# A hybrid decoder layer: the set-up, the order of the sample's queries, two planner numbers, one place of the memory change and the last pass are rewritten

## The chip, the core and the metric

The kernel runs on one core of one Trainium2 chip. The metric is the device time of one execution in microseconds (us). The kernel before took 823.68 us, the median of three runs (823.04 to 825.53). The profile is of another execution of the same program.

The engines are named as the profile names them: PE is TensorE with its matmuls (PEld its weight loads), DVE is VectorE, ACT ScalarE, POOL GpSimd, SP SyncE, which here only issues transfers. A name with q behind it (SPq) is that engine's sequencer.

## The reference, cut to what matters

One step of one layer for 512 prompt tokens and, at the same time, for 8 sample sequences of 4 new tokens each, which look back on 4096 cached tokens. All of it is fp32.

```python
hn = rms_norm(x, norm_mix)                      # x: 512 or 32 rows of 1024
z = hn @ w_in                                   # 1024 x 2560: q, k, v, u, gv of 512 each
q, k = rms_norm(z[:, q], q_gain), rms_norm(z[:, k], k_gain)     # groups of 64
att = softmax_1(q k) v - lam * softmax_2(q k) v # causal; the sample reads its cache through page_table
mix = gelu(u) * (tril(w_spatial) @ rms_norm(gelu(gv), gv_gain) + b_spatial)
h = x + concat(rms_norm(att, subln_gain) * (1 - lam_init), mix) @ w_out
y = h + square(relu(rms_norm(h, norm_ffn) @ w_up)) @ w_down     # D_FF 4096
```

Outputs are y for prompt and sample, and the new k, v and gv rows.

## The kernel before, in words

**Number format.** PE multiplies in a reduced fp32 (`fp32r`). For full precision each weight tile of 512 x 256 (512 KB, called raw when it lands) is split by `w_conv` (L265) into a high part (`wh`, a copy on ACT) and a low part (`wl`, a subtraction on DVE), and the activations are kept as `Thi` and `Tlo`; each product is three matmuls, high by high, high by low, low by high. The 32 sample rows, packed as high and low side by side in `spk`, go through PE in "packed" matmuls of 64 rows. Raw tiles are asked for by `w_issue`, at most `RAWB` = 3 ahead in a list written out beforehand; `w_get` hands out the next split pair. The first four weights are the two halves (512 of the 1024 rows each) of the two q pieces.

**Stages.** `setup` (L395) loads, builds the identity `idt` and small index columns, computes the page indices `idxK`, and issues the first two gathers of the key cache. `in_proj` (L836) multiplies ten column pieces of 256, two each for q, k, v, u, gv; for each it goes through the four prompt tiles of 128 tokens (`optB`, 12 matmuls of 256 columns for one tile and one weight half) and the packed sample. Before the first piece each prompt tile has to be multiplied by the gain (`x_gain`, L715), transposed on PE (8 transposes of 128 x 128) and split (`x_tile`, L718). Prompt attention follows inside the later pieces and behind them, then the output projection, then the feed-forward net in eight groups of 512 columns (`ffn`, L1153): the prompt runs alone through the first five (groups 0 to 4), the sample joins for the rest. `second_phase` (L117) gives the memory of the cache part to more weight buffers; before, it is called between groups 3 and 4. `finish` (L1236) transposes a result of 256 columns back and scales the rows.

**The sample's cache** runs beside all that. 64 chunks of keys and 64 of values are gathered by POOL's indirect transfers into two raw key buffers (`kraw`, 1 MB each) and four value buffers. `k_tr` (L563) transposes a key chunk on DVE into `kt` and issues the gather of the chunk two further on; `scores` (L583) multiplies it with the zero-padded queries `qz`, which `qz_fill` (L572) fills once per sample; softmax and the product with the values follow `LAG` chunks later.

**What sets the order.** The list `micro` (L670 to L698) holds these cache steps with weights, and `pump` (L703) calls them as the main work advances: each `yield` in the main work gives a cost, and `TAU` (L700) is the cost of one unit. `ATTW` (L36) is the cost that one step of prompt attention gives. Within this written order a scheduler may still shift instructions; under `pinned(True)` (L384) every engine keeps the written order, without it DVE and PE may move an instruction by at most 28 places, and POOL keeps it always. Each engine then executes its own list strictly in order; a matmul, copy or gather waits for what it needs while everything behind it on that engine waits too. `keep_warm` (L389) issues matmuls on the identity whose result nobody reads.

Of the kernel before, what the change touches and what calls it, by code (L numbers as in the profile page):

```python
# [35 lines left out]
ATTW = 2.4  # L36
# [26 lines left out]
def kernel(  # L63
# [88 lines left out]
    wq = big.tile([128, 4 * T], F32R, tag="r3", name="wq")[:, 0:2048].rearrange("p (s k c) -> p s k c", s=2, k=4)  # L152
# [4 lines left out]
    xg = [R[0][:, 1024 * t:1024 * t + 1024] for t in range(2)]  # L157
# [77 lines left out]
    for g in range(NG):  # L235
        add(group_pieces(g), [wo_pieces()] if g == G1 - 1 else [group_pieces(j) for j in samples(g)] if g >= G1 else (),
            2 if g == NG - 1 else 1)
# [27 lines left out]
    def w_conv():  # L265

        i = st["done"]
        if raws:
            raw = raws.pop(0)
            if i == 3:  # L270
                hi, lo = wq[:, 0], wq[:, 1]
            else:
                pool = pools["w"] if i % 5 > 2 else wp
                hi = pool.tile([128, 4, 256], F32R, tag="wh", name="wh")
                lo = pool.tile([128, 4, 256], F32R, tag="wl", name="wl")
# [119 lines left out]
    def setup():  # L395
        kt0 = kvp.tile([128, 4096], F32, tag="kt", name="kt0")
        xs = kt0[0:32, 0:1024]
        gm = kvp.tile([128, 1024], F32, tag="pp", name="gm")
        fg = kvp.tile([128, 2048], F32, tag="v", name="fg", bufs=VB)
        junk = kvp.tile([128, 512], F32, tag="om", name="junk")  # L400
        ptb = zt_().bitcast(I32).rearrange("p (n q) -> p n q", q=4)
# [11 lines left out]
        for t in range(1, 4):  # L413
            SP.dma_start(out=xt[t], in_=xp[:, t, :])

        G.memset(mhalf, -0.5)
        for t in ssb + [cst]:
            G.memset(t, 1.0)
        kw = dict(base=0, channel_multiplier=0, allow_small_or_imprecise_dtypes=True)
        G.iota(pf[:, 7:8], pattern=[[0, 1]], base=0, channel_multiplier=1, allow_small_or_imprecise_dtypes=True)  # L420
        make_identity(nc, idt)
# [7 lines left out]
        G.memset(gsrc[0:32, :], 0.0)  # L429


        pinned(True)
        for half in range(2):
# [13 lines left out]
        for k in range(8):  # L447
            PE.transpose(ps[:, 32 * k:32 * k + 32], xsg[:, 128 * k:128 * k + 128], idt[:32, :32])
# [969 lines left out]
```

## Time and profile before

| | |
|---|---|
| median of three runs | 823.68 us (823.04 to 825.53) |
| the profiled execution | 822.46 us |
| its span, first to last instruction | 820.7 us |
| PE busy | 797.2 us, 97% |
| DVE busy | 536.3 us, 65% |
| ACT busy | 359.9 us, 44% |
| POOL busy | 181.6 us, 22% |
| HBM | 266 GB/s over the span |

The durations in this document come from the one profiled execution. Its span is what the views divide up; the rest of its time lies around the span. A window's row gives the busy time of each engine in that stretch. A timeline row gives the start and the length of one instruction, or of a run of like ones (x16 is sixteen), and in brackets how long the engine was idle before it and what released it. PEclk is the clock that PE was granted, as a share of full speed. Names are output <- inputs; `d` is a PSUM tile, `r` a prompt tile, `a` the hidden activations, `mix` and `acc` the running sums.

### The profile page before, as it was taken

To read this page: it belongs to the slowest core of one execution; us is meant where nothing else is said; L and a number is where in the kernel's file an instruction comes from. 1 tells how busy PE (TensorE), PEld (TensorE's weight loads), DVE (VectorE), ACT (ScalarE), POOL (GpSimd) and SP (SyncE) were. 2 spreads that over 40 slices of the span, in tenths; PEclk is the share of its full clock that TensorE was granted. 3 is DMA by queue.
4 is the path that set the end of the run, shared out by engine and by line. 5 is a ranking of instruction groups with operands and counts; after the bars stand their busy time and mean duration, and the time that the engine had idled before them with its cause. 6 is when DMAs were issued, how large, how long until landed. Compare 5 with 4: busy or idle time off the path is not lost.

```text
span 820.7 us, 15362 instructions
## 1 busy us (share of the span) xinstructions
PE 797.2 (97%) x6210; PEld 632.2 (77%) x6210; DVE 536.3 (65%) x883; ACT 359.9 (44%) x892; POOL 181.6 (22%) x196
## 2 busy tenths in 40 slices
PE   6899999999999999999999999999999999999997
PEld 5788888776667788867767766666766899998997
DVE  5878776899988765796667667535644444344354
ACT  4643744785665723842352153263332431331331
POOL 4553532235332222132123122220100000000000
PEclk9999999999999999999999999999999999999999
DMA  8598698898998789859989897793696377576102
GB/s 296 208 402 288 228 352 317 317 344 307 355 333 342 290 292 343 315 201 336 371 314 342 305 376 291 257 341 115 217 285 199 116 240 234 187 237 212 59 14 97
DMA packets 101797, 219.05 MB, mean 267 GB/s; under 512 B 6089, under 2 KB 83998, under 8 KB 85342
## 3 DMA queue, kind: packets, MB, share of 16 engines
q0 software_dynamic: 18432, 134.23, 42.6%
q1 hardware_dynamic: 83294, 83.84, 31.3%
q8 instruction: 49, 0.80, 0.4%
q14 instruction: 22, 0.18, 0.1%
HBM read 213.53 MB, written 4.52 MB: 266 GB/s over the span
## 4 chain that ended last, share of the span: by engine, by line
PE 73%; DVE 10%; DMA 7%; ACT 5%; issue 2%; POOL 1%; SPq 0%; DVEq 0%; ACTq 0%; POOLq 0%
PE d L52 63%; PE O L52 5%; DMA kraw<-in_cache_k_dram,idxK 5%; PE S L52 5%; DVE kt L52 4%; ACT PT L52 2%; DMA raw<-in_w_down_dram 1%; DVE zn L52 1%; DMA kt<-in_w_in_dram 1%; DVE Tlo L52 1%; ACT z L52 1%; ACT wh L52 1%; ACT t L52 1%; DVE wl L52 1%; POOL ssb L52 0%
## 5 line engine op out<-in xcount | busy, mean ns | idle before, releaser
L52 ACT CAST wh<-raw 128x1024 fp32r<-128x1024 f32 x90 | 94.1, 1047 | 194.4 <-PE d L52 170.4
L52 PE MATMUL d<-a,wh 128*128 128x272 f32 (+1 forms) x704 | 167.0, 340 | 0.0
L52 DVE STREAM_TRANSPOSE kt<-kraw 128x2048 f32<-128x2048 f32 x64 | 146.3, 2297 | 12.4 <-PE S L52 7.5
L52 DVE TENSOR_TENSOR wl<-raw,wh 128x1024 fp32r<-128x1024 f32 x90 | 109.5, 1219 | 57.1 <-ACT wh L52 56.4
L52 PEld LDWEIGHTS d<-a,wh 128*128 128x128 f32 x704 | 113.1, 188 | 24.6 <-issue 5.4
L52 PE MATMUL d<-wh,Thi 128*128 128x256 f32 x432 | 127.7, 296 | 1.1 <-ACT z L52 0.6
L52 POOL DMA_INDIRECT v<-in_cache_v_dram,idxK x64 | 65.7, 1027 | 257.6 <-PE O L52 247.4
L52 PE MATMUL d<-wl,Thi 128*128 128x256 f32 x432 | 122.1, 283 | 0.0
L52 PE MATMUL d<-wh,Tlo 128*128 128x256 f32 x432 | 121.7, 282 | 0.2 <-DVE Tlo L52 0.2
L52 PE MATMUL d<-Thi,wh 128*128 128x272 f32 (+2 forms) x368 | 108.7, 336 | 0.0
L52 PE MATMUL d<-Tlo,wh 128*128 128x272 f32 (+2 forms) x368 | 106.5, 330 | 1.4 <-DVE Tlo L52 1.4
L52 PE MATMUL d<-Thi,wl 128*128 128x272 f32 (+2 forms) x368 | 106.4, 329 | 0.0
L52 PE MATMUL d<-a,wl 128*128 128x272 f32 (+1 forms) x352 | 102.6, 336 | 0.0
L52 POOL DMA_INDIRECT kraw<-in_cache_k_dram,idxK x64 | 70.8, 1107 | 102.3 <-DVE kt L52 54.6
L52 PEld LDWEIGHTS d<-wh,Thi 128*128 128x128 f32 x432 | 81.5, 189 | 9.9 <-issue 6.9
L52 PEld LDWEIGHTS d<-wh,Tlo 128*128 128x128 f32 x432 | 81.6, 189 | 0.4 <-DVE Tlo L52 0.4
L52 PEld LDWEIGHTS d<-wl,Thi 128*128 128x128 f32 x432 | 81.4, 188 | 0.4 <-issue 0.4
L52 PEld LDWEIGHTS d<-Thi,wh 128*128 128x128 f32 x368 | 63.5, 188 | 18.2 <-issue 7.5
L52 ACT COPY PT<-d 32x128 f32<-32x128 f32 x256 | 65.6, 256 | 14.9 <-DVE d L52 11.6
L52 PEld LDWEIGHTS d<-Tlo,wh 128*128 128x128 f32 x368 | 63.6, 188 | 7.4 <-DVE Tlo L52 1.6
L52 PEld LDWEIGHTS d<-Thi,wl 128*128 128x128 f32 x368 | 63.5, 188 | 6.2
L52 PEld LDWEIGHTS d<-a,wl 128*128 128x128 f32 x352 | 60.1, 188 | 6.9
(270 smaller groups left out, 1067.2 us busy)
## 6 DMA issues: line engine op xcount, KB each, us to landing
raw<-in_w_up_dram SPq DMA_DIRECT2D x32, 512.0 KB
raw<-in_w_down_dram SPq DMA_DIRECT2D x32, 512.0 KB
plain<-in_w_up_dram SPq DMA_DIRECT2D x20, 512.0 KB
plain<-in_w_down_dram SPq DMA_DIRECT2D x20, 512.0 KB
raw<-in_w_in_dram SPq DMA_DIRECT2D x18, 512.0 KB
raw<-in_w_out_dram SPq DMA_DIRECT2D x8, 512.0 KB
plain<-in_w_out_dram SPq DMA_DIRECT2D x8, 512.0 KB
r<-in_x_prompt_dram SPq DMA_DIRECT2D x4, 512.0 KB
```

Of the source, the lines that this page charges most:

```text
L52: r = f(*args, **kw)
```

## The change

Six things change.

1. **Set-up.** Prompt tile 0 and the first two weights are loaded first, then the sample rows, tile 1, the page table, tiles 2 and 3 and two more weights (two of them into a part of memory of their own, `w23`). The gain comes as an 8-row block that PE transposes (`gcol`), instead of a 512-KB broadcast. `x_half` transposes first and multiplies by the gain behind it, for tile 0 in four ACT copies per half, for the others in one DVE multiply per half. The first q piece goes tile by tile (both weight halves of a tile, then the next tile), each tile prepared inside the loop; the sample rows are prepared there too (`sample_in`), the seven constants on POOL later (`constants`), and the fourth weight has no buffer of its own any more.
2. **First cache chunks.** `k_tr(0)` and `k_tr(1)` are called in the second piece; the sample's q statistics run per piece instead of for both.
3. **Queries one slot sooner.** `qz_fill` moves from the first score step of a sample to the slot before it.
4. **Weight.** `ATTW` 2.4 becomes 1.6, the base in `TAU` 101.5 becomes 105.2.
5. **Memory change inside a group.** `second_phase` is called between the two halves of group 4's first part instead of ahead of group 4, and the weight list is shifted to match.
6. **Last pass in halves.** The last 256 columns go through all matmuls of the first 272 tokens, then the other 272, and are finished by halves; `finish` puts the two token tiles of a store into PSUM tiles of their own.

```diff
-ATTW = 2.4
+ATTW = 1.6
...
-            if i == 3:
-                hi, lo = wq[:, 0], wq[:, 1]
-            else:
-                pool = pools["w"] if i % 5 > 2 else wp
...
+            pool = pools["w"] if i % 5 > 2 else wp
...
     def setup():
...
-        SP.dma_start(out=xs, in_=xs_d)
-        SP.dma_start(out=ptb, in_=page_table.rearrange("b l -> (b l)").unsqueeze(0).to_broadcast([128, 256]).rearrange("p (n q) -> p n q", q=4))
-        SP.dma_start(out=gm, in_=norm_mix.to_broadcast([128, 1024]))
+        SP.dma_start(out=xt[0], in_=xp[:, 0, :])
...
+        SP.dma_start(out=grow[0:8, :], in_=norm_mix.rearrange("a (k p) -> (a k) p", p=128))
         w_issue()
         w_issue()
-        SP.dma_start(out=xt[0], in_=xp[:, 0, :])
-        for o in (1024, 3072):
-            w_issue(kt0[:, o:o + 1024].rearrange("p (k c) -> p k c", k=4))
+        SP.dma_start(out=xs, in_=xs_d)
+        SP.dma_start(out=xt[1], in_=xp[:, 1, :])
+        SP.dma_start(out=ptb, in_=page_table.rearrange("b l -> (b l)").unsqueeze(0).to_broadcast([128, 256]).rearrange("p (n q) -> p n q", q=4))
+        SP.dma_start(out=xt[2], in_=xp[:, 2, :])
+        SP.dma_start(out=xt[3], in_=xp[:, 3, :])
+        for o in (0, 1024):
+            w_issue(w23[:, o:o + 1024].rearrange("p (k c) -> p k c", k=4))
...
+        x_half(0, 0)
         w_conv()
...
+        x_half(0, 1)
+        keep_warm(10)
         w_conv()
+        indices(ptb)
...
     def scores(m):
         b, pj = divmod(m, 4)
-        if pj == 0:
-            qz_fill(b)
...
+        if n % 8 == 1 and n < NCH:
+            a.append((qz_fill, (n // 8,)))
...
-    TAU = (101.5 + 44.8 * G1 + 30.0 * ATTW) / sum(w for w, _ in micro)
+    TAU = (105.2 + 44.8 * G1 + 30.0 * ATTW) / sum(w for w, _ in micro)
...
+    def x_half(t, hf):
+        ps = dt_()
+        for k in range(4):
+            kk = 4 * hf + k
+            PE.transpose(ps[:, 128 * k:128 * k + 128], xt[t][:, 128 * kk:128 * kk + 128], idt)
...
+        if t == 0:
+            for k in range(4):
+                A.activation(out=xg[:, k], in_=psv[:, k], func=ACTF.Copy, scale=gcol[:, 4 * hf + k:4 * hf + k + 1])
+        else:
+            V.tensor_tensor(out=xg, in0=psv, in1=gcol[:, 4 * hf:4 * hf + 4].unsqueeze(2).to_broadcast([128, 4, 128]),
+                            op=ALU.mult)
+        split(xg, 4 * hf, t)
...
+        def first_pass(half, t):
+            if half == 0 and t < 3:
+                x_tile(t + 1)
+            if half == 1:
+                if t < 2:
+                    keep_warm(3)
+                x_stat(t, [xt[t]], 128, junk, G)
+            if t == 0 and half == 1:
+                sample_in(xs)
+                x_stat(4, [xs], 32, junk, G)
+            if t == 2 and half == 1:
+                constants()
+            if t == 3 and half == 0:
+                gcols(gsrc)
...
+                steps = [(h, t) for t in both for h in range(2)] if pi == 0 else [(h, t) for h in range(2) for t in both]
...
+                    if pi == 1 and half == 0:
+                        if t < 2:
+                            k_tr(t)
+                        kv["on"] = t >= 2
...
+            if switch and pr == 1:
+                while kv["i"] < len(micro):
+                    pump(1.0)
+                second_phase()
...
+    def last_pass(rng):
+        hiw, low = w_get()
+        for q, (a, e) in enumerate(rng):
+            for d in range(2):
...
+                ps = dt_()
+                for ff in range(4):
+                    for w, (st_w, mv) in enumerate(((hiw, ahi), (hiw, alo), (low, ahi))):
+                        mm(ps[:, 0:e - a], st_w[:, ff, dc], mv[ff][:, a:e], ff == 0 and w == 0, ff == 3 and w == 2)
+                V.tensor_tensor(out=acc[m][:, a:e], in0=acc[m][:, a:e], in1=ps[:, 0:e - a], op=ALU.add)
...
+                if q == 1 and d == 0:
+                    finish_rows(3, 0)
+        finish_rows(3, 1)
+        finish_sample(3)
```

How the instructions stand now, at three places. First DVE in the start. Before, around the first key chunks (`kt<-kraw` is `k_tr`, `Tlo` the low part of half a prompt tile, `zn` and `rows` the sample's queries):

```order
L52 TENSOR_REDUCE cst<-z 32x4
L52 TENSOR_TENSOR zn<-d,zn 32x256
L52 TENSOR_SCALAR zn<-zn,cst 32x256
L52 TENSOR_REDUCE cst<-z 32x4
L52 TENSOR_TENSOR Tlo<-d,Thi 128x4x128 x2
L52 STREAM_TRANSPOSE kt<-kraw 128x4x16x32
L52 TENSOR_TENSOR zn<-zn,cst 32x256
L52 TENSOR_TENSOR zn<-zn,qg 32x256
L52 STREAM_TRANSPOSE rows<-zn 32x256
```

Now the same engine around its first key chunks (`r_87<-d,gcol` is the gain multiply of half a prompt tile, `z<-d,gcol` that of the sample rows, `spk` their packing):

```order
L52 TENSOR_TENSOR wl<-w_134,wh 128x1024
L52 TENSOR_TENSOR Tlo<-r_87,Thi 128x4x128
L52 TENSOR_TENSOR r_87<-d,gcol 128x512
L52 TENSOR_TENSOR Tlo<-r_87,Thi 128x4x128
L52 TENSOR_TENSOR z<-d,gcol 128x256
L52 STREAM_TRANSPOSE kt<-kraw 128x4x16x32
L52 TENSOR_TENSOR spk<-z,spk 128x8x32
L52 TENSOR_REDUCE ssb_119<-z 128x4
L52 TENSOR_TENSOR r_87<-d,gcol 128x512
L52 STREAM_TRANSPOSE kt<-kraw 128x4x16x32
L52 TENSOR_TENSOR Tlo<-r_87,Thi 128x4x128
```

The first key transpose stood behind the sample's two statistics; it now stands ahead of the sample's packing, and the second one ahead of the low part of tile 2.

Second POOL in the start. Before, from the first gathers to the rsqrt of the sample's q statistics (`cst<-cst,mhalf 32x8`):

```order
L52 DMA kraw<-in_cache_k_dram,idxK 128x2048 x2
L52 MEMSET qz 128x512
L52 MEMSET strip 128x120
L52 MEMSET ones 128x128
L52 MEMSET z 128x128
L52 AFFINE_SELECT z<-z 128x128
L52 CAST cab<-z 128x128
L52 CAST idb<-idt 128x128
L52 TENSOR_TENSOR cst<-s 128x1
```

Now the piece that ends with the rsqrt of the first q piece (`cst<-cst,mhalf 32x4`):

```order
L52 TENSOR_SCALAR cst<-cst 128x1
L52 TENSOR_TENSOR cst<-cst,mhalf 128x1
L52 TENSOR_SCALAR rst_118<-cst 128x1
L52 MEMSET qz 128x512
L52 MEMSET strip 128x120
L52 MEMSET ones 128x128
L52 MEMSET z 128x128
L52 AFFINE_SELECT z<-z 128x128
L52 CAST cab<-z 128x128
L52 CAST idb<-idt 128x128
L52 TENSOR_SCALAR cst<-cst 32x4
L52 TENSOR_TENSOR cst<-cst,mhalf 32x4
```

The constants stood right behind the first gathers; they now stand behind the row statistics of tile 2 (the three rows on top) and directly ahead of the sample's rsqrt.

Third PE at the very end. Before (`wh`, `wl` are the last weight, `d<-idt,mix` the transposes of the result, those of 32 rows the sample's):

```order
L52 MATMUL d<-a_4341,wh 128x272 x4
L52 MATMUL d<-a_4341,wl 128x272 x2
L52 MATMUL d<-a_4341,wh 128x272 x4
L52 MATMUL d<-a_4341,wl 128x272 x2
L52 MATMUL d<-idt,mix 32x128
L52 MATMUL d<-idt,mix 128x128 x5
L52 MATMUL d<-idt,mix 32x128
L52 MATMUL d<-idt,mix 128x128 x3
```

Now:

```order
L52 MATMUL d<-idt,mix 128x128 x4
L52 MATMUL d<-a_4238,wh 128x272 x2
L52 MATMUL d<-a_4238,wl 128x272
L52 MATMUL d<-a_4238,wh 128x272 x2
L52 MATMUL d<-a_4238,wl 128x272
L52 MATMUL d<-a_4239,wh 128x272 x2
L52 MATMUL d<-a_4239,wl 128x272
L52 MATMUL d<-a_4239,wh 128x272 x2
L52 MATMUL d<-a_4239,wl 128x272
L52 MATMUL d<-idt,mix 128x128 x2
L52 MATMUL d<-idt,mix 32x128
L52 MATMUL d<-idt,mix 128x128 x2
```

All ten transposes stood behind the last matmul; four of them now stand ahead of the last twelve matmuls.

## Rows read from the trace of the kernel before

**Rows 1.** Windows: length; busy PE, PEld, DVE, ACT, POOL; PEclk; DMA share; GB/s.
```profile
0.00:40.00 40.00, 28.47 (x180) 26.47 (x180) 29.16 (x50) 22.43 (x48) 19.18 (x43) 0.96 0.70 249
40.00:800.00 760.00, 753.32 (x5909) 590.96 (x5909) 497.90 (x813) 334.62 (x838) 162.42 (x154) 1.00 0.76 273
800.00:820.70 20.70, 15.41 (x126) 14.80 (x124) 9.27 (x22) 2.81 (x6) 0.00 (x0) 0.99 0.29 96
200.00:250.00 50.00, 48.56 (x395) 33.03 (x394) 45.42 (x86) 29.61 (x94) 18.89 (x19) 1.00 0.94 355
```

**Rows 2.** Timeline of PE, 0 to 50 us: start, length, instruction, [idle before <-releaser].
```profile
3.36 3.62 PE L52 MATMUL d<-idt 128*128 128x128 f32 x16
...
21.06 1.31 PE L52 MATMUL d<-idt,r 128*128 128x128 f32 x8 [4.28 <-DVE r L52]
...
23.87 1.69 PE L52 MATMUL d<-wq,spk 128*64 128x256 f32 x8
...
26.19 0.36 PE L52 MATMUL d<-wh,Thi 128*128 128x256 f32 x1
...
29.14 0.60 PE L52 MATMUL d<-idt,r 128*128 128x128 f32 x4
...
40.34 1.93 PE L52 MATMUL S<-kt,qz 128*32 128x256 f32 x32
...
47.89 0.40 PE L52 MATMUL d<-wq,Thi 128*128 128x256 f32 x2
```

**Rows 3.** Window of 22 to 23 us.
```profile
22.00:23.00 1.00, 1.00 (x6) 1.00 (x5) 1.00 (x6) 0.90 (x2) 0.82 (x4) 0.50 1.03 422
```

**Rows 4.** Timeline of all engines, end of the span.
```profile
814.01 0.79 DVE L52 TENSOR_TENSOR mix<-mix,d 128x272 f32<-128x272 f32 x2 [0.72 <-PE d L52]
...
816.44 0.47 ACT L52 ACTIVATE t<-d,cst 128x256 f32<-128x256 f32 x1 [0.30 <-DVE t L52]
```

**Rows 5.** Timeline of ACT, start.
```profile
9.46 1.04 ACT L52 CAST wh<-raw 128x1024 fp32r<-128x1024 f32 x1 [4.95 <-DMA raw<-in_w_in_dram]
...
16.39 1.07 ACT L52 CAST Thi<-d 128x512 fp32r<-128x512 f32 x2 [1.60 <-issue]
```

**Rows 6.** Timeline of DVE, start.
```profile
10.54 1.23 DVE L52 TENSOR_TENSOR wl<-raw,wh 128x1024 fp32r<-128x1024 f32 x1 [1.26 <-ACT wh L52]
...
13.20 1.12 DVE L52 TENSOR_SCALAR idxK<-z,pf 32x64 int32<-32x64 int32 x4
...
30.95 2.30 DVE L52 STREAM_TRANSPOSE kt<-kraw 128x2048 f32<-128x2048 f32 x1
...
42.90 2.31 DVE L52 STREAM_TRANSPOSE kt<-kraw 128x2048 f32<-128x2048 f32 x1 [0.26 <-DMA kraw<-in_cache_k_dram,idxK]
```

**Rows 7.** Timeline of POOL, start.
```profile
1.57 0.28 POOL masks.py:199 TENSOR_SCALAR_AFFINE_SELECT idt<-idt 128x128 f32<-128x128 f32 x1
...
14.62 2.04 POOL L52 DMA_INDIRECT kraw<-in_cache_k_dram,idxK  x1 [8.94 <-DVE idxK L52]
...
17.90 0.55 POOL L52 MEMSET qz<- 128x512 f32 x1
...
19.91 1.16 POOL L52 CAST cab<-z 128x128 bf16<-128x128 f32 x1
...
23.56 0.25 POOL L52 TENSOR_SCALAR rst<-cst 128x1 f32<-128x1 f32 x1
...
29.91 1.68 POOL L52 TENSOR_TENSOR cst<-cst,mhalf 32x8 f32<-32x8 f32 x1
33.53 1.09 POOL L52 DMA_INDIRECT kraw<-in_cache_k_dram,idxK  x1 [1.95 <-DVE zn L52]
```

**Rows 8.** Chain of waits, 30 to 50 us.
```profile
38.42 6.86 DMA kraw<-in_cache_k_dram,idxK
```

**Rows 9.** DMA queues, 18 to 20 us: packets, MB, share of 16 engines.
```profile
q0 software_dynamic: 1, 0.01, 1.1%
```

**Rows 10.** DMA queues, 20 to 22 us.
```profile
q0 software_dynamic: 90, 0.74, 91.5%
```

More of the change, by code (lines that the diff above doesn't have):

```diff
@@ L235 @@
     for g in range(NG):
-        add(group_pieces(g), [wo_pieces()] if g == G1 - 1 else [group_pieces(j) for j in samples(g)] if g >= G1 else (),
+        add(group_pieces(g), [[[], [], [], sum(wo_pieces()[0:2], []), sum(wo_pieces()[2:4], [])]] if g == G1 - 1 else [group_pieces(j) for j in samples(g)] if g >= G1 else (),
             2 if g == NG - 1 else 1)
@@ L474, in setup, with sample_in @@
         G.tensor_copy(out=idb, in_=idt)
-        return gm, F, gsrc, junk
+    def sample_in(xs):
+        ps = dt_()
+        for k in range(8):
+            PE.transpose(ps[:, 32 * k:32 * k + 32], xs[:, 128 * k:128 * k + 128], idt[:32, :32])
+        xsg = zt_()
+        sv = xsg.rearrange("p (k t) -> p k t", k=8)
+        V.tensor_tensor(out=sv, in0=ps[:, 0:256].rearrange("p (k t) -> p k t", k=8),
+                        in1=gcol[:, 0:8].unsqueeze(2).to_broadcast([128, 8, 32]), op=ALU.mult)
+        pack(sv, 0, 8)
     def masks(F, gsrc):
@@ L885, in in_proj @@
             items = []
[L886 to L889 removed]
+            A_, B_ = w_get(), w_get()
             for tp in range(2):
@@ new lines, in in_proj @@
+                both = (2 * tp, 2 * tp + 1)
+                steps = [(h, t) for t in both for h in range(2)] if pi == 0 else [(h, t) for h in range(2) for t in both]
+                for half, t in steps:
+                    w = (A_, B_)[half]
+                    cost = next(att, 0.0) if 2 * pi + tp >= ATT0 else 0.0
+                    if half == 0:
+                        pss[t] = dt_()[:, 0:256]
+                    optB(pss[t], t, *w, half)
+                    if t == 3 or (pi == 0 and t == 2 and half == 1):
+                        w_conv()
+                    if t % 2 == 1:
+                        flush()
+                    if pi == 0:
+                        first_pass(half, t)
+                    if half == 1:
+                        post(kind, p, t, pss[t], 128, ss, items)
+                        if pi == 4 and t == 0:
+                            params()
+                        if pi == 4 and t == 3:
+                            params2()
+                        if pi == 9 and t > 0:
+                            cat_tile(t - 1)
+                        if t == 3 and items:
+                            finish_piece(kind, p, ss, items)
+                        if pi == 0 and t == 1:
+                            pinned(False)
+                    elif pi == 5:
+                        next(nt, None)
+                    if pi == 1 and half == 0:
+                        if t < 2:
+                            k_tr(t)
+                        kv["on"] = t >= 2
+                    if pi == 1 and t == 0 and half == 1:
+                        masks(F, gsrc)
+                        load_params()
+                    yield 1.3 + cost
+                    if tp == 0 and t == 1:
@@ L1151, in h_split, with ffn @@
                                op1=ALU.subtract)
-    def ffn(start, joint, last, small):
+    def ffn(start, joint, last, small, switch=False):
         rng = [(0, 272), (272, 544)] if joint else [(0, 512)]
@@ L1208, in ffn @@
                 yield 2.8
-            step()
+            if pr or not switch:
+                step()
         for dp in range(4):
+            if last and dp == 3:
+                yield from last_pass(rng)
+                return
             hiw, low = w_get()
@@ L1227, in ffn @@
             step()
+            if switch and dp == 1:
+                step()
             if last and dp == 0:
```

186 lines of the change are left out of this document (58 added, 128 removed).

## Prediction

> **What bounds the kernel now.** I read three windows and one dense one first [rows 1]: from 40 to 800 us TensorE (PE) is busy 753.3 of 760, in the first 40 only 28.5, in the last 20.7 only 15.4. The number of real matmuls does not change, so another order can win at most these 23.5 us without a matmul and what PE does slowly; half of it lies in the first 40. The densest stretch of attention, 200 to 250, loses 1.4 us with VectorE (DVE) at 45.4 of 50. So the reader should look at the two ends. At the start PE's own timeline [rows 2] shows a gap of 4.28 us before 21.06, the first prompt matmul at 26.19, the first cache scores at 40.34 and, at 47.89, the first matmul with the second weight half of the second q piece. I call that last place M and measure the start by it. The clock row [rows 3] gives the second cost of a gap: after the idle stretch PE was granted 0.50 of full speed, the 1.2 GHz level, and eight packed matmuls at 23.87 took 1.69 us, while 24 prompt matmuls from 26.19 to 29.14 took 0.12 each; the low level lasted some 5 us from 21.06. At the other end the last adds begin at 814.01, and the span closes at 820.7 [rows 4].
>
> **The start, step by step.** The change puts prompt tile 0 and two weights first, takes the broadcast gain (512 KB) out, and scales behind the PE transposes instead of in front of them. The removed DVE work is one 32x1024 and two 128x1024 multiplies before PE needs them; the added work is one 512-column multiply for each half tile.
>
> First, when do the cache gathers leave? They need the page indices, which stand behind the second weight on DVE both times. ScalarE (ACT) now has in a row: four scaled copies of 128 columns, a 512-column cast, a weight cast, and the same three again. A 512-column cast takes 0.53 us (two in 1.07) and a weight cast 1.04 [rows 5]; the 128-column copy is not in the trace, and lies between a quarter of 0.53 and 0.53; I take 0.27, so 2 x (4 x 0.27 + 0.53 + 1.04) = 5.3 us (bounds 4.2 to 7.4). The fifth load in the old queue was there at 9.46 [rows 5]; tile 0, now first, I estimate at 6 (5 to 8), its transposes done at 6.8. That gives 12.1, plus 1.2 for the subtraction and 1.1 for the indices [rows 6]: 14.4. Before, the first gather left at 14.62 [rows 7]. The reordering gains nothing for the gathers.
>
> Second, what waits for them? In the new order the transpose of the first cache tile (STREAM_TRANSPOSE) stands on DVE *in front of* the sample rows' packing, and that of the second in front of tile 2's low part; before, both stood behind all of this. DVE runs in order, so PE's packed sample matmuls, and the rest of tile 1 queued behind them, wait for a gather. Two later gathers bound its duration: one issued at 38.42 landed 6.86 us later, one issued at 33.53 was waited for until 42.90, 9.4 us [rows 6 to 8]. The latter is the nearest, the first of a pair, so the first tile is there at 14.4 + 9.4 = 23.8 and the second some 2.5 later. Bounds: 21.3 (6.86), and above 30.95, since the old transpose began there without a wait and shows only that the tile had come by then.
>
> Third, from there to M. DVE: 2.3 us of transpose [rows 6] and 0.4 of packing (a third of a 1.23-us subtraction), so PE resumes at 26.5, having run out of work at about 19. At the low clock 8 packed (1.7), 12 prompt matmuls (2.6) and three dummy ones (1.0; 0.45 each at 3.36 [rows 2], half of that when the clock is back) end at 31.8; 8 packed and 12 prompt matmuls at full speed (0.95 + 1.43) at 34.2; the transposes of tile 3 go out at 34.5. Tile 3's two multiplies and subtractions with 1.1 us of small work between them bring its low half to 37.4 on DVE, PE finishes tile 3 at 40.0 and the first weight half of the second piece with 24 matmuls at 42.9. Meanwhile GpSimd (POOL) must finish the statistics of tile 2 (from 37.0, after ACT's squares) and seven constants before the sample's rsqrt: those eleven instructions took 5.9 us from 17.90 to 23.8 [rows 7], and at their shortest some 3.2 (the two 1.2-us casts at the 0.28 of a like select on an idle core). I take 3.9, nearer the short end because DVE has little to do beside them, then 1.2 for the rsqrt (1.68 for twice the columns, and a small add) and 2.3 on DVE (three head operations and the fourth weight's subtraction): M at 44.4 (43.7 to 46.4). By M the old program had done more: 32 records of scores (1.93), eight packed matmuls (0.95) and small transposes, 3.2 us. The start is worth 47.89 - 44.4 - 3.2 = 0.3 us. The head start is real, about 15 us at the first prompt matmul, and is given back to a wait.
>
> Here the row shows casts of 1.16 us with DVE at work beside them, and a select of 0.28 when DVE was idle [rows 7]. The Trainium skill, "SBUF — State Buffer", section "SBUF: two separate sides", says that DVE and GpSimd take a shared port pair as an exclusive lock, so the loser blocks for a whole instruction. By that rule the constants run short here, because DVE mostly waits at that moment: M at 43.7 and the start worth 1.0; by the long row it is worth -1.7.
>
> **The other edits.** The tail: before, after the last matmul came two adds (0.79 for both), the transposes, and a DVE and an ACT scaling one after the other, the last ending at 816.91, then the output [rows 4]. Now the first token half is added, transposed and scaled under the last 12 matmuls; what remains is one add (0.45), transposes and the latency before the scaling (0.7), and two scalings side by side from separate PSUM tiles (0.47). PE has 4 transposes more in front (0.4): 814.4 + 0.45 + 0.7 + 0.47 = 816.0, 0.9 earlier. The last large store then shares the queue with a 32 KB one instead of a second 256 KB one: 0.1 (0 to 0.6). Tail 1.0 (0.6 to 1.5). Weight 1.6 and the TAU base: PE's gaps in the middle come to 6.7 us in 760 [rows 1]; moving a slot can remove or add one, 0 (-1.5 to 1.5). The queries' fill one slot sooner: DVE work of about 0.5 us for each sample, off the path, 0; if its cover goes, 0.5 eight times over at most, which the windows [rows 1] speak against. The memory change inside group 4: the last cache product and the first plain weight are 25 us of matmuls apart instead of 37, and the merge of the sample's halves lies under them; 0 (-1 to 0.5; without that cover up to the 12 us that were taken away). The fourth weight now goes into the common pool and waits for the first one's last matmul: covered by tile 3, counted in M. Sum of the forecast: 0.3 + 1.0 = 1.3 us.
>
> **The rivals.**
> 1. *The gather's wait is short, and the change is faster.* If the first tile lands at 21.3, all steps to M move 2.5 us, and if the gap before it then is too short to cost the clock, another 2.4. With the short constants' time the start is worth 3 to 6, with the tail 4 to 7 us. For it: the hardware queue has 0.5 MB less in front of the gathers. Against it: while that queue was full, from 18 to 20 us, the gather queue moved one packet, and 90 in the next two [rows 9, 10]. The Trainium skill, "DMA: Bandwidth & Descriptors", section "SWDGE vs HWDGE vs iDMA", states that each DMA engine alternates between the software and hardware queues; by that rule the gather would share from the moment it is ready and land about a microsecond sooner, which the packet rows here do not show. I take 5 us: 817.5 in the profiled execution, 818.7 as a median.
> 2. *The gather's wait is long, and the change is slower.* The same place, DVE's first cache transpose. Every microsecond of landing after 23.8 is one on M, as nothing else of PE's is left. It decides for slower from about 27.6 (3.8 late, less the 1.3 of the forecast). For it: the old trace excludes nothing before 30.95, and one pair of tiles moves 2 MB with three weights in the same queue. Against it: the later gathers of 6.9 and 9.4 us. At 29 us: 5.2 late, 3.9 lost: 826.4, or 827.6 as a median.
> 3. *The tail does not move*, because the last 32 KB store, issued behind the large one, lands last: the forecast less 1.0, still within what cannot be told apart.
>
> **How the numbers follow.** The profiled execution took 822.46, its span 820.7, so 1.8 us lie around it; the median of the three runs, 823.68, is 1.2 above it. Forecast: 822.46 - 1.3 = 821.2 in the profiled execution's terms, 822.4 as a median; its own range 820 to 825. A measurement of this kernel tells from no change what exceeds 0.3%, 2.5 us. Forecast with rival 3: 0.43, of which 0.05 reaches faster; rival 1: 0.30; rival 2: 0.27, of which 0.02 stays within. So faster 0.35, the same 0.40, slower 0.25. The range reaches into both rivals: 817.5 to 827.
>
> **What would show it.** Right: on DVE a wait of 3 us or more for the first cache tile, ending near 24, directly followed by the sample packing; a PE gap of about 7 us ending near 26.5 with a granted clock of 0.5 behind it; M near 44.4; the last scaling ending about 2.0 us after the last matmul instead of 2.9. Wrong in step 1: the first gather before 13 or after 16. Wrong in step 2: no wait on DVE before the first cache transpose (rival 1) or one beyond 27 (rival 2). The whole argument fails if PE shows gaps of several us after 50 us, which none of the terms holds.

## The result, and the profile after

The changed kernel took 832.17 us, the median of four runs (830.29 to 835.72); the kernel before took 823.51 in the same measurements. The ratio is 1.0106 [1.0083, 1.0129]: 8.7 us slower, outside the predicted range, and none of the prediction's rivals names its cause. The profiled execution took 832.17, its span is 830.4 (before: 820.7).

Where the 9.7 us of span went is read from windows. The columns are those of [rows 1]. First before (its first 40 us stand in [rows 1]), then after, cut at the same places:

```profile
40.00:160.00 120.00, 118.28 (x1132) 99.40 (x1132) 90.59 (x168) 63.38 (x182) 48.93 (x40) 1.00 0.86 317
160.00:330.00 170.00, 167.88 (x1480) 126.68 (x1479) 140.30 (x247) 99.77 (x293) 56.66 (x59) 1.00 0.88 327
330.00:660.00 330.00, 327.16 (x2054) 236.53 (x2053) 205.35 (x292) 132.34 (x298) 56.82 (x56) 1.00 0.77 274
```

```profile
0.00:40.00 40.00, 31.48 (x227) 29.21 (x227) 23.77 (x48) 23.22 (x52) 13.11 (x47) 0.96 0.64 218
40.00:160.00 120.00, 109.46 (x986) 93.87 (x987) 81.73 (x150) 56.50 (x156) 45.19 (x39) 0.96 0.75 267
160.00:330.00 170.00, 165.35 (x1445) 125.75 (x1444) 137.86 (x258) 102.56 (x309) 50.63 (x54) 1.00 0.81 299
330.00:660.00 330.00, 328.01 (x2102) 231.91 (x2100) 217.28 (x300) 132.47 (x304) 68.02 (x67) 1.00 0.82 301
```

PE's idle time is the length less the busy time. In the first 40 us it fell by 3.0 us. From 40 to 160 it rose from 1.7 to 10.5, and the granted clock there is 0.96 instead of 1.00; from 160 to 330 it rose by 2.5. Behind 330 us nothing more is lost. Over the whole span PE is idle 6.1 us longer (29.6 against 23.5) and busy 3.6 us longer (800.8 against 797.2), with more of its work at the lower clock: that is the 9.7. So the reader has to look at 40 to 160. PE's timeline of the changed kernel (start, length, instruction, idle time before and its releaser):

```profile
9.51 0.39 PE L52 MATMUL d<-wh,Thi 128*128 128x256 f32 x1 [0.48 <-ACT wh L52]
...
24.05 0.30 PE L52 MATMUL d<-wh,spk 128*64 128x256 f32 x1 [1.60 <-DVE spk L52]
...
41.80 0.28 PE L52 MATMUL d<-wh,Thi 128*128 128x256 f32 x1
...
64.41 3.64 PE L52 MATMUL S<-kt,qz 128*32 128x256 f32 x32 [3.02 <-DVE qz L52]
...
105.98 0.35 PE L52 MATMUL d<-s,Rm 128*128 128x4 f32 x2 [2.44 <-DVE s L52]
...
113.47 1.93 PE L52 MATMUL S<-kt,qz 128*32 128x256 f32 x32 [1.25 <-ACT P L52]
```

Against [rows 2]: the first prompt matmul stands at 9.51 instead of 26.19, the place M at 41.80 instead of 47.89. But the first cache scores stand at 64.41 instead of 40.34, and they and the first sample's softmax (`d<-s,Rm`) make PE wait. Two stretches around and behind these waits have half the clock, the 1.2 GHz level:

```profile
63.30:70.10 6.80, 5.69 (x42) 3.73 (x43) 4.15 (x8) 0.00 (x0) 1.19 (x1) 0.50 0.43 156
107.70:111.10 3.40, 3.40 (x18) 3.40 (x17) 3.40 (x4) 1.07 (x2) 1.04 (x1) 0.50 0.22 47
```

What the waits wait for is on DVE and POOL. DVE first:

```profile
63.30 0.76 DVE L52 TENSOR_TENSOR zn<-zn,ssb 128x256 f32<-128x256 f32 x2 [3.35 <-POOL ssb L52]
63.98 0.48 DVE L52 TENSOR_TENSOR qz<-qrep,mh 128x128 f32<-128x128 f32 x2
...
104.87 0.42 DVE L52 TENSOR_TENSOR zn<-zn,ssb 128x256 f32<-128x256 f32 x1 [3.39 <-POOL ssb L52]
105.21 0.15 DVE L52 TENSOR_TENSOR s<-s 128x1 f32<-128x1 f32 x1
```

```profile
60.34 2.93 POOL L52 TENSOR_TENSOR ssb<-ssb,mhalf 128x16 f32<-128x16 f32 x1
...
101.26 3.57 POOL L52 TENSOR_TENSOR ssb<-ssb,mhalf 128x20 f32<-128x20 f32 x1
```

Each piece of q and k ends with such an rsqrt on POOL, of 2.9 to 3.6 us, and on DVE the scaling `zn` waits for it. A cache step that stands behind that scaling on DVE (`qz`, the first sample's queries; `s`, its maxima) waits with it, though it needs nothing from it, and PE waits for the cache step. Before, the first sample's maxima fell between two such scalings, and PE's matmul on them had no wait. DVE before, then PE:

```profile
68.67 0.72 DVE L52 TENSOR_TENSOR zn<-zn,ssb 128x256 f32<-128x256 f32 x2
...
77.91 0.10 DVE L52 TENSOR_TENSOR s<-s 128x1 f32<-128x1 f32 x1
...
86.88 0.76 DVE L52 TENSOR_TENSOR zn<-zn,ssb 128x256 f32<-128x256 f32 x2 [2.18 <-POOL ssb L52]
```

```profile
79.69 0.28 PE L52 MATMUL d<-s,Rm 128*128 128x4 f32 x2
```

### The profile page after: what moved, and what is told of

The parts are those of the page before. It is cut to its first block, busy times and chain, and to the rows that moved or that the text cites. A ratio compares the mean times of both kernels' runs of the same rounds, so it can differ in the third digit from the quotient of the medians.

```text
span 830.4 us, 15410 instructions
## 1 busy us (share of the span) xinstructions
PE 800.8 (96%) x6229; PEld 633.6 (76%) x6229; DVE 535.7 (65%) x887; ACT 360.4 (43%) x900; POOL 176.9 (21%) x206
## 4 chain that ended last, share of the span: by engine, by line
PE 70%; issue 9%; DVE 7%; ACT 5%; DMA 5%; POOL 4%; SPq 1%; DVEq 0%; POOLq 0%; ACTq 0%
PE d L52 60%; PE S L52 5%; PE O L52 4%; DVE kt L52 2%; DMA kraw<-in_cache_k_dram,idxK 2%; ACT PT L52 2%; POOL ssb L52 2%; DMA w<-in_w_in_dram 1%; DMA v<-in_cache_v_dram,idxK 1%; SPq L52 1%; DMA gg<-in_lambda_q_dram 1%; DVE wl L52 1%; DVE zn L52 1%; POOL v L52 1%; ACT z L52 1%
## 5 line engine op out<-in xcount | busy, mean ns | idle before, releaser
L52 PE MATMUL d<-a,wh 128*128 128x272 f32 (+1 forms) x704 | 168.7, 341 | 0.0
L52 DVE STREAM_TRANSPOSE kt<-kraw 128x2048 f32<-128x2048 f32 x64 | 146.4, 2297 | 17.7 <-PE S L52 12.6
L52 PE MATMUL d<-wh,Thi 128*128 128x256 f32 x448 | 133.7, 299 | 4.5 <-ACT Thi L52 2.3
L52 PE MATMUL d<-wl,Thi 128*128 128x256 f32 x448 | 128.1, 286 | 0.9 <-DVE wl L52 0.9
L52 PE MATMUL d<-wh,Tlo 128*128 128x256 f32 x448 | 127.6, 285 | 0.8 <-DVE Tlo L52 0.8
L52 PEld LDWEIGHTS d<-wh,Thi 128*128 128x128 f32 x448 | 85.9, 192 | 13.3 <-issue 4.3
L52 POOL DMA_INDIRECT kraw<-in_cache_k_dram,idxK x64 | 68.2, 1065 | 99.7 <-DVE kt L52 63.9
L52 PEld LDWEIGHTS d<-wh,Tlo 128*128 128x128 f32 x448 | 85.9, 192 | 1.1 <-DVE Tlo L52 1.0
L52 PEld LDWEIGHTS d<-wl,Thi 128*128 128x128 f32 x448 | 85.7, 191 | 1.3 <-DVE wl L52 1.3
L52 PE MATMUL S<-kt,qz 128*32 128x256 f32 x1024 | 64.4, 390 | 4.8 <-DVE qz L52 3.0
```

The lines of the kernel that those rows point to most:

```text
L52: r = f(*args, **kw)
```

## The experiments

All ratios are to the kernel before, measured beside each experiment; times of different experiments are best compared by these ratios. There are 18 experiments. Each profile is of one execution. L is the theory that the cache chain (the sample's cache steps in their order) is simply too late, P that its phase, which step of it meets which step of the main work, makes the loss. The other letters are explained where they are used first.

**Which part.** e1 to e4 take the parts of the change apart, e8 adds the partner that was missing. e1 has sections 1 and 2 of the change and nothing else. e2 is the changed kernel with

```diff
-ATTW = 1.6
+ATTW = 2.4
...
-    TAU = (105.2 + 44.8 * G1 + 30.0 * ATTW) / sum(w for w, _ in micro)
+    TAU = (101.5 + 44.8 * G1 + 30.0 * ATTW) / sum(w for w, _ in micro)
```

e3 is the kernel before with sections 4 to 6 of the change, e4 with section 6 alone, e8 with sections 5 and 6; their lines are those of the diff above.

> The kernel before with the new set-up and first pass alone; queries' slot, weight 2.4 with base 101.5, memory change and last pass are as before. The changed kernel's PE idles 10.9 us between 40 and 160 us, against 1.7 before. Theory S (set-up): the sample's queries and the gathers of key chunks 2 and 3 come some 10 us later, the scores 24 us later, and PE waits for the cache steps: this kernel shows these waits too, 9 us or more idle between 40 and 160, and takes 831 to 835 us. Theory W (weight and base): the cache steps are only planned against the wrong place, so this kernel idles 2 to 4 us there and, with the 3.4 us that the first 40 us gained, takes 819 to 823 us.

845.71 us, 1.0247 [1.0212, 1.0282]. More than theory S said: set-up and key chunks alone cost 22 us, and sections 3 to 6 give most of it back.

> The changed kernel with the weight back at 2.4 and the base at 101.5, all else as changed. Theory S: the late cache chain stays, 829 to 833 us, and the first scores still stand near 64 us. Theory W: the waits between 40 and 160 us go from 10.9 to some 2 to 4, 822 to 825 us.

836.67 us, 1.0151 [1.0122, 1.0180]. Theory W falls: with the new set-up the weight and base do not lose, they win 4.5 us by the medians (the interval just overlaps that of the changed kernel). e2 has sections 3, 5 and 6 over e1 and is 9.0 us faster.

> The kernel before with weight 1.6 and base 105.2, the memory change inside the group and the last pass in halves; set-up and the queries' slot as before. Theory S: nothing is late, and the last pass gives its 1.8 us: 820 to 823. Theory W: the planner's numbers alone put 8 to 10 us of waits between 40 and 330 us, 829 to 832.

828.69 us, 1.0067 [1.0041, 1.0092]. Theory S missed as well: without the new set-up the same numbers lose.

> The kernel before with the last pass in halves alone. In the changed kernel the time from the end of the last feed-forward matmul to the end of the span went from 6.6 to 4.8 us. Both theories: 1.8 us less than before, 821.5 to 822.2. If the gain in the changed kernel was an accident of its other order, no difference.

822.62 us, 0.9986 [0.9968, 1.0004]: 1.0 us, the interval just reaches no change.

> The kernel before with the memory change inside the group and the last pass in halves, weight 2.4 and base 101.5, the planner on from the first piece as before. It is the partner of e7 with the chain at its old place, and of e3 with the old weight. Theory L and rival S2 alike: 821 to 824 us. If the memory change itself costs (against the prediction's 0), 825 or more; what e3 has above this kernel is then the price of the weight and base, by 5 us if the memory change is free.

821.58 us, 0.9984 [0.9967, 1.0002]. The memory change is free. e3 stands 7.1 us above it: that is the price of weight 1.6 with base 105.2 in the old set-up, while in the new one they were a gain of 4.5. The parts don't add; something that both of them move has to decide.

**Is it the place of the cache chain?** e5 is the changed kernel with the key chunks called earlier, e7 the old set-up with the planner switched on late (and sections 3, 5 and 6).

```diff
+            if t == 1 and half == 1:
+                k_tr(0)
+            if t == 2 and half == 0:
+                k_tr(1)
             if t == 2 and half == 1:
                 constants()
...
                     if pi == 1 and half == 0:
-                        if t < 2:
-                            k_tr(t)
                         kv["on"] = t >= 2
```

> The changed kernel with k_tr(0) and k_tr(1) called in the first piece (behind tile 1, ahead of the constants) instead of in the second: on VectorE the sample's packing then stands ahead of both cache transposes, and GpSimd issues the gathers of chunks 2 and 3 near 33 us instead of at 43.6 and 48.2. The prediction's term (a wait of VectorE for the first gather, and late gathers) says: PE's gap of 1.6 us before the packed matmuls goes, the later gathers come earlier, 828 to 831 us. Lateness theory (L: the first scores stand 24 us later because the planner is switched on one and a half pieces later, and the first scores wait for the queries, not for the keys): the first scores stay near 64 us, the waits between 40 and 160 us stay near 11, 830.5 to 833.

833.61 us, 1.0135 [1.0117, 1.0152]. The scores stayed at 64.15 with a wait of 3.04 us. The late gathers of chunks 2 and 3 are not the cause.

```diff
             k_tr(1)
-            kv["on"] = True
...
+                        if pi == 1 and half == 0:
+                            kv["on"] = t >= 2
```

> The old set-up with weight 2.4 and base 101.5, the memory change, the queries' slot and the last pass as changed, but the planner of the cache steps switched on where the changed kernel does it (second half of the second piece instead of before the first). It is the kernel e2 with the old set-up. Theory L: the place of the chain alone makes the loss: first scores at 58 to 66 us, 8 or more us of idle time between 40 and 160, 830 to 838 us. Rival S2: with the old set-up nothing waits, 820 to 825 us.

833.09 us, 1.0123 [1.0107, 1.0138]: 11.5 us above e8, and a wait of 4.02 us for the first softmax at 105.15. The place at which the planner is switched on costs that much with the old set-up, together with the queries' slot of section 3, which e8 does not have; the two were not taken apart. So far L holds.

**Does an early chain bring it back?** e6 is the changed kernel with the sample's part of the second q piece computed behind that of the first and the planner switched on there; the masks are made in the first piece, too, the fourth weight has its own buffer, and the base is 117.4. e9 is e6 with weight 2.4 and base 101.5, e10 is e9 with the queries' transposes put off.

```diff
+                            sq0 = combine(sps)
+                            st0 = head_stat(sq0[0:32], 32, cst[0:32, 0:4], 4)
+                            sps = dt_()[0:64, 0:256]
+                            for hf in range(2):
+                                packed(*cvt[hf], [(4 * hf + b, b) for b in range(4)], sps, hf == 0, hf == 1)
...
+                            k_tr(0)
+                            k_tr(1)
+                            kv["on"] = True
```

> The changed kernel with the sample's part of the second q piece done right behind that of the first, both key chunks and the masks prepared in the first piece, the planner switched on there (base 117.4 for the one piece more), and the fourth weight in a buffer of its own again. Theory L: the first scores stand near 42 to 48 us, PE's idle time between 40 and 160 us falls from 10.9 to 2 to 5, 821 to 826 us. Rival S2 (the waits come from the new set-up's crowded engines, not from the place of the chain): the idle time in 40 to 160 stays at 8 or more, 829 us or more.

829.92 us, 1.0078 [1.0065, 1.0090]. The first scores moved from 64.4 to 52.8 only, and PE is idle 9.5 us between 40 and 160. 2.3 us came back by the medians, and the interval overlaps that of the changed kernel: no clear gain.

> e6 (new set-up, both q pieces' sample part and the planner in the first piece) with the weight at 2.4 and the base at 101.5 again. Theory L with the weight's price tied to the chain's place (e3 stood 7.1 us above e8 with the chain early; with the chain late the same numbers won 4.5): the early chain wants the old numbers, 821 to 824.5 us, with 1 to 4 us of idle time between 75 and 330 us instead of 11. If the price of the weight belongs to the old set-up alone: 828 us or more.

835.01 us, 1.0133 [1.0106, 1.0161]. This speaks against L: the numbers are the old ones, the first scores (52.38) stand 12 us ahead of the changed kernel's, and it is not faster. They still stand 12 us behind the old 40.34, so L does not fall by it.

```diff
-                            q_sample(0, st0, cst[0:32, 0:4])
-                            q_sample(1, st1, cst[0:32, 4:8])
+                            later(lambda a=st0, b=st1: (q_sample(0, a, cst[0:32, 0:4]), q_sample(1, b, cst[0:32, 4:8])))
```

> e9 with the transposes of the sample's queries put off by two steps, so that PE's prompt matmuls stand ahead of them; in e6 PE waited 4.3 us for those queries at 44.85. That wait goes if there is work to put in front: 2 to 4 us less than e9, 818 to 821 us, the fastest so far. If the wait only moves to the scores: as e9 within 1 us.

835.65 us, 1.0143 [1.0113, 1.0172]. The wait of 3.5 us for the queries became one of 1.4 for the scores and one of 2.6 behind them.

**Is it single waits, or the numbers?** e11 and e13 take one wait out of the changed kernel each: e11 fills the first queries in `sample_q`, e13 moves the first softmax one step. e12 is e8 with a smaller weight at the same cost of one unit.

```diff
-        if n % 8 == 1 and n < NCH:
+        if n % 8 == 1 and 1 < n < NCH:
...
                 q_sample(p, zs, sc)
+                if p == 1:
+                    qz_fill(0)
```

> The changed kernel with the fill of the first sample's queries called right behind the second q piece's queries instead of by the planner, so that on VectorE it stands ahead of the scaling that waits for GpSimd's rsqrt. PE's wait of 3.0 us before the first scores at 64.4 goes, and with it the 6.8 us at half clock behind it (some 3.4 us): 825.5 to 828.5. If the wait costs only itself, 829; if it only moves to the next step of the chain, 831 to 832.5.

831.67 us, 1.0083 [1.0059, 1.0107]. The wait at 64 is gone, and one of 3.13 us stands at 60.90 (`<-ACT z`).

```diff
+    micro[16] = (0.05, micro[16][1])
+    micro[19] = (0.55, micro[19][1])
```

> The changed kernel with the first sample's softmax planned one step (1.45 units of cost) earlier, later slots unmoved: on VectorE its maxima then stand ahead of the scaling that waits for GpSimd's 3.57 us rsqrt. Theory P (phase: the loss comes from single cache steps that fall behind such a rsqrt wait on an engine that runs in order): PE's wait of 2.44 us at 106 and the 3.4 us at half clock behind it go, 827 to 829.5. Rival M (a moved wait comes back at the next step): 831 to 833.

834.62 us, 1.0130 [1.0108, 1.0151]. The wait at 106 is gone, the next score step waits 2.90 us for ACT's exponentials instead of 1.25. That is rival M, the moved wait comes back at the next step. How much e13 is slower than the changed kernel says little of the moved step: in its profile the first key gather came 2.3 us later (see below), and the first scores stand at 68.27 instead of 64.41.

```diff
-ATTW = 2.4
+ATTW = 1.6
...
-    TAU = (101.5 + 44.8 * G1 + 30.0 * ATTW) / sum(w for w, _ in micro)
+    TAU = (125.5 + 44.8 * G1 + 30.0 * ATTW) / sum(w for w, _ in micro)
```

> e8 (old set-up, memory change, last pass) with the weight 1.6 and the base 125.5, so that the cost of one unit of cache work stays what it was, and only the attention steps count less. e3 had both, the weight and 5 per cent denser cache work, and stood 7.1 us above e8. If the density makes the price: 821 to 823.5. If the smaller weight in attention does: 826 to 830.

819.70 us, 0.9942 [0.9919, 0.9964]: faster than before, and than e8 by 1.9. e3 differs from it in the base alone, 5 per cent denser cache work, and is 9.0 us slower. That L cannot explain: nothing is late in e3, whose first softmax stands at 78.69 without a wait, in e12 at 80.96.

**Phase.** e16 is e12 with the whole chain half a piece later, e15 the new set-up with the chain moved to the steps at which e12 has it, e14 the same without that.

```diff
             kv["on"] = True
+            kv["t"] = -6.0
```

> e12 (old set-up) with 6.0 units taken off the planner's count at its start: every cache step half a piece later against the main work, nothing else. Theory P: it loses like the kernels with the new set-up, 826 to 834, with a wait of 2 to 4 us of PE for the first softmax. Theories S and D: 819 to 822.

837.63 us, 1.0167 [1.0144, 1.0190]: 17.9 us from one number. PE idles 17.9 us from 40 to 660 us, in e12 7.8. The mean granted clock does not tell the two apart: it was 0.980 to 0.991 in e16's runs and 0.987 to 0.998 in e12's, whose times lie within 2.1 us. The first softmax's wait in e16, by PE, POOL and DVE:

```profile
91.20 0.35 PE L52 MATMUL d<-s,Rm 128*128 128x4 f32 x2 [4.55 <-DVE s L52]
```

```profile
82.70 3.56 POOL L52 TENSOR_TENSOR ssb<-ssb,mhalf 128x20 f32<-128x20 f32 x1
```

```profile
86.30 0.76 DVE L52 TENSOR_TENSOR zn<-zn,ssb 128x256 f32<-128x256 f32 x2 [3.98 <-POOL ssb L52]
...
90.47 0.12 DVE L52 TENSOR_TENSOR s<-s 128x1 f32<-128x1 f32 x1
```

The maxima stand behind the scaling, which waits for the rsqrt, and behind a key transpose of 2.3 us that follows it. In e12 the same maxima stand ahead of that scaling:

```profile
79.10 0.12 DVE L52 TENSOR_TENSOR s<-s 128x1 f32<-128x1 f32 x1
...
88.23 0.76 DVE L52 TENSOR_TENSOR zn<-zn,ssb 128x256 f32<-128x256 f32 x2 [2.18 <-POOL ssb L52]
```

> e10 (new set-up, both q pieces' sample part in the first piece, queries deferred) with the numbers of e12 (weight 1.6, base 125.5), the planner switched on behind tile 1 as in e10, so 6.0 units of cost (about half a piece) later against the main work than in e12. Control for the next. Theory P: as e9 and e10, 828 to 836. Theory D (e12's numbers are good in themselves): 817 to 822.

844.56 us, 1.0255 [1.0232, 1.0277]. Theory D falls: e12's numbers are not good in themselves.

```diff
+            if pi == 1:
+                kv["t"] += 6.0
```

> e14 with 6.0 units added once to the planner's count at the second piece, so that from there on every cache step stands against the same step of the main work as in e12; set-up new. Theory P: the waits at 92 and 102 us and those behind 170 go, idle time between 40 and 330 us falls to 5 to 9, 815 to 821. Theory S (the new set-up itself crowds the engines): 826 or more.

831.73 us, 1.0096 [1.0075, 1.0117]: the phase gave 12.8 us, but not the whole way to e12. Why is seen by laying PE's waits side by side, e12 first, then e15:

```profile
178.91 0.44 PE L52 MATMUL d<-idt,t 128*128 128x128 f32 x2 [0.71 <-ACT t L52]
...
216.64 0.55 PE L52 MATMUL d<-idt,t 128*128 128x128 f32 x3 [1.09 <-DVE zn L52]
...
236.86 0.66 PE L52 MATMUL d<-idt,t 128*128 128x128 f32 x4 [1.18 <-DVE osum L52]
...
268.90 0.33 PE L52 MATMUL d<-idt,mix 128*128 128x128 f32 x1 [0.78 <-DVE mix L52]
```

```profile
48.12 3.64 PE L52 MATMUL S<-kt,qz 128*32 128x256 f32 x32 [4.76 <-DVE qz L52]
...
68.06 1.94 PE L52 MATMUL d<-idt,zn 128*128 128x128 f32 x8 [6.25 <-DVE zn L52]
...
190.92 0.44 PE L52 MATMUL d<-idt,t 128*128 128x128 f32 x2 [0.69 <-ACT t L52]
...
229.08 0.55 PE L52 MATMUL d<-idt,t 128*128 128x128 f32 x3 [1.49 <-DVE zn L52]
...
248.84 0.66 PE L52 MATMUL d<-idt,t 128*128 128x128 f32 x4 [1.08 <-DVE osum L52]
...
280.90 0.33 PE L52 MATMUL d<-idt,mix 128*128 128x128 f32 x1 [0.78 <-DVE mix L52]
```

From 179 us on the two kernels wait at the same instructions, for the same engines, 12.0 to 12.4 us apart: with the phase equal, the middle is equal, whatever the set-up was. The 12 us are lost before: M stands at 41.77 in e15, 6.2 ahead of e12 (47.97), and then come the two waits on top, with work at the lower clock around them (0.80 on average from 40 to 75):

```profile
40.00:75.00 35.00, 23.99 (x205) 19.82 (x207) 19.46 (x27) 11.77 (x25) 23.52 (x30) 0.80 0.88 328
```

DVE's rows of e15 for the two waits:

```profile
47.77 0.29 DVE L52 TENSOR_TENSOR qz<-qrep,mh 128x128 f32<-128x128 f32 x1 [1.51 <-POOL qz L52]
...
63.83 2.31 DVE L52 STREAM_TRANSPOSE kt<-kraw 128x2048 f32<-128x2048 f32 x1 [4.32 <-DMA kraw<-in_cache_k_dram,idxK]
```

The first ends with 1.5 us for the queries' buffer, which POOL clears too late (the constants); until 46.2 DVE was at the queries themselves and two weight subtractions. The second is for a DVE that itself waits for a key gather and has the scaling `zn` queued behind it. In e14, half a piece later, PE waits 1.54 and 2.61 at these two places: with e12's phase the chain asks for queries and keys sooner than the new set-up has them.

**The clock behind a wait.** e17 fills e12's gap of 4.28 us before 21.14 with matmuls that nobody reads, e18 is e12 again.

```diff
         x_gain(gm, 2)
+        keep_warm(32)
         x_tile(1)
```

> e12 with 32 matmuls on the identity in PE's 4.28 us gap before the transposes of tile 1 (0.12 us each, 3.7 us in all, so they end ahead of the gap's end). In the rows of before and of e12 the gap is followed by 3.4 us at half clock. If the idle time is what makes the clock fall: no half clock there, 1.0 to 1.7 us less than e12 in the same call. If the clock falls for another reason: the same as e12.

> e12 once more, on the same chip as e17: 819 to 820.5 us, below the kernel before by 0.4 to 0.7 per cent.

e18: 820.39 us, 0.9935 [0.9912, 0.9958], as e12. e17: 822.49 us, 0.9969 [0.9953, 0.9985]. A window of e12 and the same of e17:

```profile
21.00:25.00 4.00, 3.86 (x20) 3.89 (x21) 4.00 (x10) 1.53 (x3) 3.74 (x7) 0.57 1.01 415
```

```profile
21.00:25.00 4.00, 4.00 (x38) 4.00 (x37) 1.78 (x5) 0.56 (x2) 2.65 (x7) 1.00 1.00 407
```

The clock stayed up where PE was kept busy, so at this place its fall came from the idle time. The time forecast for e17 was missed all the same: one such matmul makes two records, and the 32 took 7.31 us, not 3.7. They ran past the end of the gap, and the kernel lost 2.1 us against e18 instead of gaining 1.0 to 1.7.

## Why the prediction was wrong, step by step

**The step that failed** is how the start was turned into time: "By M the old program had done more", priced as 3.2 us of matmuls still owed, together with "Weight 1.6 and the TAU base [...] 0 (-1.5 to 1.5)". The first books late cache steps as work that is merely done later, the second books a moved slot as a small matter of either sign. With M as it was measured, 41.80, the prediction's own sum would be 47.89 - 41.80 - 3.2 = 2.9 us for the start and 1.0 for the tail, 3.9 us faster; the kernel was 8.7 slower. The 12.6 us between lie behind M: in these two terms, or in the queries' slot, which was put at 0. The runs showed in their place that the phase of the cache steps decides: 17.9 us between e12 and e16, 9.0 between e12 and e3, 11.5 between e8 and e7 (with the queries' slot), each with the set-up unchanged. The sentence that "The whole argument fails if PE shows gaps of several us after 50 us" named the symptom; no term and no rival held it. The few gaps in the old middle (6.7 us in 760, [rows 1]) were taken as a property of the work, while e16 has the same work and idles 10 us longer there than e12.

**The first gather.** It left at 14.69 (forecast 14.4). DVE's wait was there but short in the profiled execution of the changed kernel, and long in that of e1, which has the same start:

```profile
21.28 2.31 DVE L52 STREAM_TRANSPOSE kt<-kraw 128x2048 f32<-128x2048 f32 x1 [0.48 <-DMA kraw<-in_cache_k_dram,idxK]
```

```profile
24.57 2.31 DVE L52 STREAM_TRANSPOSE kt<-kraw 128x2048 f32<-128x2048 f32 x1 [4.56 <-DMA kraw<-in_cache_k_dram,idxK]
```

In e1 PE's gap before the packed matmuls is 7.26 us and ends at 27.34: the forecast (7 us, 26.5) met that execution, the lower bound of the landing (21.3) met the other. In e2, e11 and e13, with the same start again, the wait was 1.27, 2.48 and 3.66. From 16 to 20 us the gathers' queue moved 128 packets in the changed kernel's profile, beside 135 of the hardware queue, and 63 in e1's, beside 522. So the mechanism was right, and its size is what varies between these executions; e5, which puts the packing in front, does not gain by it, because the loss is elsewhere.

**M.** 41.80 against 44.4: 2.5 of the 2.6 us are the gather's. The seven constants and the four instructions in front of them took 3.5 us (34.47 to 37.98; forecast 3.9). The lower bound of 3.2 does not come out of its own working: 5.9 less some 0.9 for each of the two casts is 4.1. The half clock behind the gap at 21.06 was read as some 5 us; it lasted 3.4, from 21.7 to 25.2. Rival 1 was thus true of the start in the profiled execution, and the kernel was slower all the same.

**The tail** fits: 1.0 by e4, though its interval touches no change, so that the gain is not clear of noise. In the changed kernel the last scaling of prompt rows ends 1.5 us after the last feed-forward matmul (825.59), where the forecast said 2.0:

```profile
825.63 0.44 DVE L52 TENSOR_TENSOR mix<-mix,d 128x272 f32<-128x272 f32 x1 [1.10 <-PE d L52]
...
826.64 0.47 ACT L52 ACTIVATE t<-d,cst 128x256 f32<-128x256 f32 x1 [1.99 <-PE d L52]
```

**The memory change** was right at 0 (e8 against e4). **The queries' slot**, put at 0, was not tried alone. e2 is 9.0 us faster than e1 by sections 3, 5 and 6, and 5 and 6 gave 2 us in the old set-up; what the slot has of the rest is open.

**What stays open.** Why one phase is better than another was shown for the first softmax only, not for all the waits; e11 and e13 show that a single removed wait comes back at another step. That the phase makes losses of this size was shown with the old set-up. In the changed kernel itself the chain was not shifted alone, and all eleven kernels with the new set-up took 829.9 us or more. So the rival that the new set-up makes part of the loss itself, by queries and gathers that come late, is not excluded; e15's two early waits speak for it. Whether some numbers let the new set-up keep its 6 us at M was not found: with e12's phase its chain asks for queries too early. The fastest version is e12, the old set-up, 0.9942 [0.9919, 0.9964].

## What to carry to other kernels

Where a side chain is woven into a main chain by a planner, a faster start of the main chain shifts the later meetings of the two. Read from the trace which slow wait of an in-order engine (here DVE's for POOL's rsqrt of 3 us) the side steps now fall behind, and expect one or two per cent (here up to 2.2). Test it with one number that shifts the side chain alone, before taking the change apart. A wait of PE can cost the half clock behind it as well, here some 3 us more for a wait of 3.0, or nothing more.

## What the runs showed of the hardware

Half clock came behind some of PE's waits and not behind others of the same length. In the changed kernel 6.8 us at 0.50 lie around and behind the wait of 3.02, and 3.4 behind that of 2.44. In e13 the first scores wait 3.03, in e11 the first softmax 2.47, and the clock behind them is 1.00 (e13, then e11):

```profile
68.27:75.00 6.73, 6.73 (x73) 5.96 (x74) 5.79 (x8) 1.21 (x3) 2.08 (x3) 1.00 0.52 172
```

```profile
106.70:113.00 6.30, 4.66 (x38) 4.41 (x38) 6.30 (x14) 2.52 (x6) 1.76 (x2) 1.00 0.50 149
```

What decides between the two was not tried.

Two small POOL instructions lasted about as long as DVE's subtraction beside them. In the changed kernel, POOL, then DVE:

```profile
37.45 0.29 POOL L52 CAST cab<-z 128x128 bf16<-128x128 f32 x1
...
40.16 1.51 POOL L52 TENSOR_SCALAR cst<-cst 128x1 f32<-128x1 f32 x1
...
42.41 1.02 POOL L52 TENSOR_SCALAR rst<-cst 128x1 f32<-128x1 f32 x1
```

```profile
40.41 1.20 DVE L52 TENSOR_TENSOR wl<-w,wh 128x1024 fp32r<-128x1024 f32 x1
...
42.11 1.23 DVE L52 TENSOR_TENSOR wl<-raw,wh 128x1024 fp32r<-128x1024 f32 x1
```

An operation on one column took 1.51 and 1.02 us while DVE's subtraction of 1.2 us ran, against 0.25 in [rows 7], and the cast that took 1.16 there took 0.29 here, with DVE at small work. The Trainium skill, "SBUF — State Buffer", section "SBUF: two separate sides", calls the port pair that the two engines share an exclusive lock for a whole instruction; it counts a DVE operation with two SBUF inputs among those that take it, against a GpSimd operation that reads SBUF. The rows agree: the subtraction has two such inputs, and the two POOL instructions read SBUF. The constants, with DVE at small work or waiting, ran shorter than before, 3.5 us with the four in front against 5.9, as the prediction took from that rule.
